# A streamed squared-ReLU down projection: where raw weight chunks, the last gain and the residual lie in SBUF

## The chip, the cores and the metric

One Trainium2 chip, one core. The metric is the time of one execution in microseconds (us): the median of three runs is 1517.41 us (1516.36 to 1518.62).

## The reference, cut to what matters

A decoder layer for 256 tokens, model width 2048, one layer, all in float32. Ahead of the part in question stand the two token mixers (an RG-LRU and a sliding-window attention), whose merged output is added to x. The part that the change touches is the MLP at the end:

```python
h = rmsnorm(x, norm_mlp_pre)                  # (256, 2048)
u = jnp.square(jax.nn.relu(h @ w_mlp_up))     # (256, 8192)
x = x + rmsnorm(u @ w_mlp_down, norm_mlp_post)
```

## The kernel before

**Float32 by halves.** TensorE multiplies a float32 product as three: every operand is split into a high part and a low part (`hi`, `lo`), and hi·hi, hi·lo and lo·hi are accumulated. The weights are read from HBM once, in chunks of 128x2048. `Stream` (`ws`) loads each chunk as two halves of 128x1024 (512 KB) on SP's queue (L76, tile `wraw`), casts the high part on ACT (L94, `whi`) and subtracts on DVE (L95, `wlo`). The raw halves go round a ring of WRAW = 4 buffers, the parts round rings of WHALF = 6. `ahead(j)` asks for the splitting of the halves up to AHEAD (6) on and for loads up to WRAW further on.

**The down projection.** The 8192 inner channels are taken in two halves f = 0, 1 (first the up projection of a half, then its down projection) and the 2048 outputs in two halves n = 0, 1. So there are four passes `down(f, n)` of 16 pairs each; pair p uses one chunk, that is two raw halves. In the first pass pair p has the halves 336 + 2p and the next: `t348`, `tlo352` are of its pairs 6 and 8; pair 0 of the second pass is 368.

An ordinary pair costs 24 matmuls of 128x512. The pairs in `SEVEN` = (0, 2, 4, 6, 8, 10, 12) are done with seven block products in place of eight, as in Strassen's method: 21 matmuls. Their chunk needs sums of its blocks beside the blocks: `split_sums` makes `t` on DVE (L123, L125, L126; L125 overwrites part of the raw half b), ACT casts `thi` (L129), DVE subtracts `tlo` (L130). `t`, `thi` and `tlo` take a room each of the pool `big`: 12 rooms of 8 KB for each partition. In the down passes of f = 0, four of them hold h2T (the input of the up projection) and five hold uT (the activations of ordinary pairs), so three are free; in those of f = 1 h2T is gone, and there are more. The activations of sevenfold pairs lie in seven slots of their own, tag `seven`, that are spent pair by pair in the very last pass.

Within a sevenfold pair TensorE takes the products in the order P1, Q3, P2, P6, Q4 (with T4), Q5 (T1), N7 (T3): the first four use the blocks themselves (12 matmuls), the last three the sums, so the first matmul that reads `tlo` is the 14th. The last two pairs of a pass are held back and finished name by name; behind each name's last matmul stands `finish`.

**The end.** The f = 0 results go to DRAM (`acc_away`) and come back as `acc` for f = 1. In the last pass (f = 1, n = 1) ACT's queue loads the last norm's gain `g3`, spread over 128 partitions (1 MB, L1232), ahead of the pass, and the residual `x1` (2 x 1 MB, L1197) in `early`, behind pair 12. `early` adds `acc` to the partial results (L1193), two of the four on POOL in that pass. `finish` adds the bank (L1210), squares with a sum on ACT (L1214, whose elementwise output goes to a room `spare` that nobody reads) and multiplies with `g3` (L1215); behind the second name of a token tile stand the rms, the update of `x1` (L1223) and the stores (L1224). L1126 is the combination of the seven products behind pair 12.

**Order.** A list scheduler, which simulates the program with costs of its own, sets the order of each engine's instructions; a tile waits for the readers of the tile that had its room or buffer before it. So the order can move wherever a room changes hands.

Of the kernel before, what the change touches and what calls it, by code (L numbers as in the profile page):

```python
# [18 lines left out]
F32 = mybir.dt.float32  # L19
F32R = mybir.dt.float32r  # L20
# [5 lines left out]
P = 128  # L26
# [27 lines left out]
class Stream:  # L54
# [11 lines left out]
    def load_to(self, n):  # L66
        while self.loaded < min(n, 2 * len(self.chunks)):
            j = self.loaded
            c = slice(j % 2 * 1024, j % 2 * 1024 + 1024)
            if j < 2 * EXTRA:  # L70
                if j % 2 == 0:
                    self.place = self.room(f"wraw{j}")
                t = self.place[:, c]
            else:
                t = self.pool.tile([P, 1024], F32, tag="wraw", bufs=WRAW, name=f"wraw{j}")
            self.nc.sync.dma_start(t, self.chunks[j // 2][:, c])  # L76
            self.raw[j] = t
            self.loaded += 1

# [87 lines left out]
def layer(tc, x, g_pre, pos_t, pos_row, inv_freq, vecs, sinks, gains, w_kv, w_q, w_xy, w_rg, w_g, w_rp, w_ap, w_out,  # L167
# [921 lines left out]

    PLACE = {(0, 0): "Q4", (0, 1): "Cs", (1, 0): "P2", (1, 1): "Q3"}  # L1090

    def down(f, n, uT, held, order, finish, early, between=lambda p: None):

        two = [pair(f"s{i}") for i in range(2)]
        banks = {name: two[i // 2][:, i % 2].rearrange("p a b -> p (a b)")
                 for i, name in enumerate(("P1", "P6", "Q5", "N7"))}
        banks.update((name, bank(psb, f"d{name}")) for name in ("P2", "Q3", "Q4", "Cs"))
        begun = set()
        v = nc.vector

        def step(p, parts, names):
            for name in names:
                at, n2 = name
                b = PLACE[name]
                for i, (hi, lo) in enumerate(parts):
                    t = slice(at * P, at * P + P)
                    c = quarter(n2)
                    a = uT[p][:, i]
                    product(banks[b], (a[:, 0, t], a[:, 1, t]), (hi[:, c], lo[:, c]), b in begun,
                            p == PAIRS - 1 and i == 1)  # L1110
                    begun.add(b)

        ready = {}
        for p in range(PAIRS - held):
            if p in SEVEN:
                parts = ws.seven()
# [24 lines left out]
            between(p)  # L1141
        parts = [[ws.half(False) for i in range(2)] for p in range(held)]
        for name in order:
            for i in range(held):
                step(PAIRS - held + i, parts[i], (name,))
            finish(name, banks[PLACE[name]], ready[name])
        ws.ahead(ws.at - 1)

    for f in range(2):
        uT = {}  # L1150
        rooms = [unit(f"uT{f}{i}") for i in range((PAIRS - len(SEVEN) + 1) // 2)]
        full = []
        for p in range(PAIRS):
            u = u2("u")
            if f == 0 and p < 2:
                up_pair(p, wide(u))
            else:
                a_pair(h2T, wide(u), PRIO if p == PAIRS - 1 else 0)
            full.append((p, u))
            if f == 0 and p == R2_AT:  # L1160
                pump(99)
                spread_r2()
                ctx3.close()
                pc = ctx2.enter_context(tc.tile_pool(name="pc", bufs=1))
            if f == 1 or p >= R2_AT:
                for q, u in full:
                    if q in SEVEN:
                        uT[q] = pc.tile([P, 2, 7, P], F32R, tag="seven", bufs=len(SEVEN), name=f"seven{f}{q}")
                    else:
                        i = sum(k not in SEVEN for k in range(q))  # L1170
                        uT[q] = rooms[i // 2][:, 2 * (i % 2) : 2 * (i % 2) + 2]
                    evacuate(q, u, uT[q])
                full.clear()
        order = [(1, 1), (1, 0), (0, 0), (0, 1)]
        if f == 0:
            for n in range(2):
# [11 lines left out]
        x1 = []  # L1188

        def early(ready):  # L1190
            for (tb, i), t in ready.items():
                c = quarter(2 * n + i)
                (nc.gpsimd if n and tb else nc.vector).tensor_tensor(t, t, acc[tb][:, c], ALU.add)  # L1193
            if n == 1:
                for tb in range(TB):
                    x1.append(flat(unit(f"x1{tb}", F32)))
                    nc.scalar.dma_start(x1[tb], x1_away[tb])  # L1197

        def between(p):
            if p in (3, 5, 7, 9):  # L1200
                tb, q = divmod((p - 3) // 2, 2)
                c = quarter(q)
                nc.vector.tensor_tensor(acc[tb][:, c], acc[tb][:, c], g3[:, c], ALU.mult)

        def finish(name, b, t):
            tb, i = name
            q = 2 * n + i
            c = quarter(q)
            a = acc[tb][:, c]
            nc.vector.tensor_tensor(a, b, t, ALU.add)  # L1210
# [3 lines left out]
            nc.scalar.activation(spare[:, c], a, AF.Square, accum_out=sq[:, 3, tb, q : q + 1])  # L1214
            nc.vector.tensor_tensor(t, a, g3[:, quarter(q)], ALU.mult)  # L1215
            last[tb, i] = t
            if i == 0:
                return
            r = rms(tb, 3)
            for q in range(4):  # L1220
                c = quarter(q)
                g = acc[tb][:, c] if q < 2 else last[tb, q - 2]
                nc.vector.scalar_tensor_tensor(x1[tb][:, c], g, r, x1[tb][:, c], ALU.mult, ALU.add)  # L1223
                (nc.scalar if q % 2 else nc.sync).dma_start(o_v[tb][:, c], x1[tb][:, c])  # L1224
# [83 lines left out]
```

## Time and profile before

| what | us |
|---|---|
| median of 3 runs | 1517.41 (1516.36 to 1518.62) |
| the profiled execution | 1517.5 |
| its span | 1515.7 |
| TensorE busy in the span | 1493.5 (99%) |
| DVE busy | 1102.2 (73%) |
| ACT busy | 829.2 (55%) |
| POOL busy | 5.5 |

The profiled execution is the slowest core's; here there is only one. Some 1.8 us lie around the span. Matmul times in the timeline are modelled and overlap (a row says 0.39 where a matmul is issued each 0.23 us), so the pace of TensorE is read from the chain of waits, whose pieces follow on each other.

### The profile page before, as it was taken

How to read it: one execution, taken by the hardware profiler on the slowest of the kernel's cores; microseconds unless marked ns; L12 is line 12 of the kernel's file. 1: busy time of each engine (PE TensorE's matmuls, PEld its weight loads, DVE VectorE, ACT ScalarE, POOL GpSimd, SP SyncE). 2: the span in 40 equal slices, each digit the busy share in tenths (PEclk: the TensorE clock that was granted, in tenths of full speed). 3: DMA queues.
4: the chain of work that ended last, by engine and by line, in shares of the span. 5: the costliest groups of instructions: out<-in, count | busy, mean ns of one | idle time of the engine just before them, and what ended most of it. 6: DMA issues, size and time to landing. Idle time of an engine off the chain costs nothing.

```text
span 1515.7 us, 20016 instructions
## 1 busy us (share of the span) xinstructions
PE 1493.5 (99%) x7600; PEld 1259.8 (83%) x7600; DVE 1102.2 (73%) x1377; ACT 829.2 (55%) x1143; POOL 5.5 (0%) x11
## 2 busy tenths in 40 slices
PE   9999999999999999999999999999999999999996
PEld 7787778788888888888888888888888888888875
DVE  6666677858769966555667866798886666688897
ACT  6554654646566766443355655555454455555543
POOL 0000000000000000000000000000000000000001
PEclk9999999999999999999999999999999999999999
DMA  6645445465646565655764756566657555566564
GB/s 253 218 144 187 142 131 170 153 196 166 217 159 215 174 209 196 191 183 194 268 225 137 271 183 193 185 203 213 219 195 239 194 188 188 193 236 213 195 209 174
DMA packets 82895, 296.19 MB, mean 195 GB/s; under 512 B 9712, under 2 KB 9968, under 8 KB 81648
## 3 DMA queue, kind: packets, MB, share of 16 engines
q1 hardware_dynamic: 79056, 284.43, 57.4%
q10 hardware_dynamic: 3744, 10.50, 1.9%
q8 instruction: 59, 0.97, 0.2%
q14 instruction: 36, 0.29, 0.1%
HBM read 288.60 MB, written 6.29 MB: 195 GB/s over the span
## 4 chain that ended last, share of the span: by engine, by line
PE 82%; DVE 9%; DMA 4%; ACT 2%; issue 2%; DVEq 0%; SPq 0%; ACTq 0%
PE ps L256 21%; PE ps L254 11%; PE dQ L1084 4%; DMA wraw<-in_w_dn 4%; PE pp L294 4%; PE pp L296 4%; PE pp L298 4%; PE g L294 3%; DVE wlo L95 3%; PE g L298 3%; PE g L296 3%; PE s L1084 3%; PE dP L1084 2%; PE q L296 2%; PE q L298 2%; PE q L294 2%
## 5 line engine op out<-in xcount | busy, mean ns | idle before, releaser
L94 ACT CAST whi<-wraw 128x1024 fp32r<-128x1024 f32 x523 | 544.6, 1053 | 567.5 <-PE ps L256 123.7
L95 DVE TENSOR_TENSOR wlo<-wraw,whi 128x1024 fp32r<-128x1024 f32 x523 | 632.8, 1221 | 301.9 <-ACT whi L94 295.2
L256 PE MATMUL ps<-h2T,whi 128*128 128x512 f32 x960 | 223.9, 390 | 0.0
L256 PEld LDWEIGHTS ps<-h2T,whi 128*128 128x128 f32 x960 | 178.2, 188 | 35.6
L256 PE MATMUL ps<-hT,whi 128*128 128x512 f32 x512 | 121.3, 391 | 0.0
L254 PEld LDWEIGHTS ps<-h2T,wlo 128*128 128x128 f32 x960 | 119.1, 192 | 2.3
L254 PE MATMUL ps<-h2T,wlo 128*128 128x256 f32 x960 | 119.9, 283 | 0.0
L256 PEld LDWEIGHTS ps<-hT,whi 128*128 128x128 f32 x512 | 94.7, 188 | 20.1 <-issue 1.5
L1084 PE MATMUL dQ<-whi,uT 128*128 128x512 f32 x288 | 106.9, 389 | 0.0
L294 PE MATMUL g<-whi,hT 128*128 128x512 f32 x256 | 101.2, 395 | 0.0
L296 PE MATMUL g<-wlo,hT 128*128 128x512 f32 x256 | 100.0, 391 | 0.1
L298 PE MATMUL g<-whi,hT 128*128 128x512 f32 x256 | 99.8, 390 | 0.0
L254 PE MATMUL ps<-hT,wlo 128*128 128x256 f32 x512 | 64.9, 283 | 0.0
L254 PEld LDWEIGHTS ps<-hT,wlo 128*128 128x128 f32 x512 | 63.8, 191 | 1.2
L1084 PEld LDWEIGHTS dQ<-whi,uT 128*128 128x128 f32 x288 | 54.1, 188 | 11.2
L1084 PE MATMUL dQ<-wlo,uT 128*128 128x512 f32 x144 | 56.4, 391 | 1.2 <-DVE wlo L95 1.1
L294 PEld LDWEIGHTS g<-whi,hT 128*128 128x128 f32 x256 | 48.1, 188 | 10.6 <-issue 1.0
L298 PEld LDWEIGHTS g<-whi,hT 128*128 128x128 f32 x256 | 48.1, 188 | 10.2
L296 PEld LDWEIGHTS g<-wlo,hT 128*128 128x128 f32 x256 | 48.1, 188 | 9.9 <-DVE wlo L95 0.5
L1084 PE MATMUL dCs<-whi,uT 128*128 128x512 f32 x144 | 54.1, 389 | 0.0
L1084 PE MATMUL dP<-whi,uT 128*128 128x512 f32 x144 | 54.1, 389 | 0.0
L130 DVE TENSOR_TENSOR tlo<-t,thi 128x1536 fp32r<-128x1536 f32 x28 | 49.2, 1756 | 5.5 <-ACT thi L129 5.3
(280 smaller groups left out, 2462.1 us busy)
## 6 DMA issues: line engine op xcount, KB each, us to landing
wraw<-in_w_up SPq DMA_DIRECT2D x128, 512.0 KB, 4.1
wraw<-in_w_dn SPq DMA_DIRECT2D x128, 512.0 KB, 4.8
wraw<-in_w_g SPq DMA_DIRECT2D x64, 512.0 KB, 4.7
wraw<-in_w_xy SPq DMA_DIRECT2D x64, 512.0 KB, 4.5
wraw<-in_w_q SPq DMA_DIRECT2D x32, 512.0 KB, 4.4
wraw<-in_w_ap SPq DMA_DIRECT2D x32, 512.0 KB, 4.6
wraw<-in_w_rp SPq DMA_DIRECT2D x32, 512.0 KB, 4.1
wraw<-in_w_out SPq DMA_DIRECT2D x32, 512.0 KB, 4.9
```

Source lines behind the costliest of these rows:

```text
L94: self.pin(self.nc.scalar.copy(hi, src))
L95: self.pin(self.nc.vector.tensor_tensor(lo, src, hi.bitcast(F32), ALU.subtract))
L130: v.tensor_tensor(lo, t, hi.bitcast(F32), ALU.subtract)
L254: mm(ps[:, f, 1, :], w, a[:, 0, :], start=False, stop=j == 1 and k == 7)
L256: mm(ps[:, f].rearrange("p a b -> p (a b)"), w, a.rearrange("p a b -> p (a b)"), start=kt == 0, stop=j == 3 and k == 7)
L294: mm(banks[tb][n], a[:, 0, t], hi[:, n * 512 : n * 512 + 512], start=first, stop=False)
L296: mm(banks[tb][n], a[:, 0, t], lo[:, n * 512 : n * 512 + 512], start=False, stop=False)
L298: mm(banks[tb][n], a[:, 1, t], hi[:, n * 512 : n * 512 + 512], start=False, stop=last)
L1084: mm(b, a[x], w[y], start=not begun and i == 0, stop=tail and i == 2)
```

## The change

Line numbers of the changed kernel are two higher from the body of `down` on (L1084 is L1086), and more at the end. The diff, cut to its core:

```diff
@@ Stream.load_to
-            if j < 2 * EXTRA:
+            if j < 2 * EXTRA or j // 2 in self.sums:
                 if j % 2 == 0:
                     self.place = self.room(f"wraw{j}")
                 t = self.place[:, c]
...
-            self.nc.sync.dma_start(t, self.chunks[j // 2][:, c])
+            self.load = self.nc.sync.dma_start(t, self.chunks[j // 2][:, c]).ins
@@ Stream.ahead
-        self.load_to(max(2 * EXTRA, j + WHALF) + WRAW)
+        n = max(2 * EXTRA, j + WHALF) + WRAW
+        self.load_to((n + 1) // 2 * 2 + 2 if (n - 1) // 2 in self.sums else n)
@@ down: a callback behind the parts of the held pairs
         parts = [[ws.half(False) for i in range(2)] for p in range(held)]
+        split()
@@ the end, f = 1
-                (nc.gpsimd if n and tb else nc.vector).tensor_tensor(t, t, acc[tb][:, c], ALU.add)
-            if n == 1:
-                for tb in range(TB):
-                    x1.append(flat(unit(f"x1{tb}", F32)))
-                    nc.scalar.dma_start(x1[tb], x1_away[tb])
+                nc.vector.tensor_tensor(t, t, acc[tb][:, c], ALU.add)
+        def free_half(name):
+            t = pc.tile([P, 2, 7, P], F32R, tag="seven", bufs=len(SEVEN), name=name)
+            return t.rearrange("p a b c -> p (a b c)")[:, 0:1024].bitcast(F32)
         def between(p):
-            if p in (3, 5, 7, 9):
+            if p in (0, 2):
+                g3.append(free_half(f"g3{p}"))
+                nc.scalar.dma_start(g3[-1], gains[3][p * 512 : p * 512 + 1024].partition_broadcast(P))
+            if p in (4, 6, 8, 10):
...
+        def residual_back():
+            for tb in range(TB):
+                for i in range(2):
+                    x1[tb, i] = free_half(f"x1{tb}{i}")
+                    with tc.issue_after(ws.load):
+                        ws.load = nc.sync.dma_start(x1[tb, i], x1_away[tb][:, i * 1024 : i * 1024 + 1024]).ins
...
-            nc.scalar.activation(spare[:, c], a, AF.Square, accum_out=sq[:, 3, tb, q : q + 1])
+            nc.scalar.activation(b, a, AF.Square, accum_out=sq[:, 3, tb, q : q + 1])
...
-        spare = flat(unit("spare", F32))
-        g3 = flat(unit("g3", F32))
-        nc.scalar.dma_start(g3, gains[3].partition_broadcast(P))
-        down(f, n, uT, 2, [(0, 0), (0, 1), (1, 0), (1, 1)], finish, early, between)
+        down(f, n, uT, 2, [(0, 0), (0, 1), (1, 0), (1, 1)], finish, early, between, residual_back)
```

In words: (1) both raw halves of a sevenfold chunk lie in one room of `big` instead of two ring buffers, and `ahead` takes such a chunk whole; (2) `g3` comes as two halves into spent `seven` slots, asked for behind pairs 0 and 2 of the last pass, and its multiplications with the first half of `acc` stand one pair later; (3) the residual comes as four loads on SP's queue behind the last weight load, into spent slots; (4) the four adds of the last `early` are all DVE's; (5) the squares' unread output goes to the PSUM bank instead of `spare`.

**Where the order moves: pairs 6 to 8 of the first down pass.** DVE's rows before, from the sums of pair 6 (`t348`) on:

```order
L123 TENSOR_TENSOR t348_8774<-wraw349_8727,wraw348_8713 128x1024
L95 TENSOR_TENSOR wlo348_8781<-wraw348_8713,whi348_8780 128x1024
L125 TENSOR_TENSOR wraw349_8727<-t348_8774,wraw348_8713 128x512
L126 TENSOR_TENSOR t348_8774<-wraw349_8727 128x512
L95 TENSOR_TENSOR wlo349_8785<-wraw349_8727,whi349_8784 128x1024
L95 TENSOR_TENSOR wlo350_8828<-wraw350_8758,whi350_8827 128x1024
L95 TENSOR_TENSOR wlo351_8832<-wraw351_8760,whi351_8831 128x1024
L130 TENSOR_TENSOR tlo348_8776<-t348_8774,thi348_8775 128x1536
L123 TENSOR_TENSOR t352_8851<-wraw353_8804,wraw352_8790 128x1024
```

The same place in the changed kernel:

```order
L95 TENSOR_TENSOR wlo348_8777<-wraw348_8710,whi348_8776 128x1024
L123 TENSOR_TENSOR t348_8770<-wraw348_8710 128x1024
L125 TENSOR_TENSOR wraw348_8710<-t348_8770,wraw348_8710 128x512
L126 TENSOR_TENSOR t348_8770<-wraw348_8710 128x512
L95 TENSOR_TENSOR wlo349_8781<-wraw348_8710,whi349_8780 128x1024
L130 TENSOR_TENSOR tlo348_8772<-t348_8770,thi348_8771 128x1536
L95 TENSOR_TENSOR wlo350_8827<-wraw350_8713,whi350_8826 128x1024
L95 TENSOR_TENSOR wlo351_8831<-wraw351_8715,whi351_8830 128x1024
L95 TENSOR_TENSOR wlo352_8853<-wraw352_8786,whi352_8852 128x1024
L123 TENSOR_TENSOR t352_8846<-wraw352_8786 128x1024
```

`tlo348` moved ahead of pair 7's low parts (350, 351), and the sum `t352` behind `wlo352`. SP's queue at that place before, in plain order of the halves:

```order
L76 DMA wraw348_8713<-in_w_dn 128x1024
L76 DMA wraw349_8727<-in_w_dn 128x1024
L76 DMA wraw350_8758<-in_w_dn 128x1024
L76 DMA wraw351_8760<-in_w_dn 128x1024
L76 DMA wraw352_8790<-in_w_dn 128x1024
L76 DMA wraw353_8804<-in_w_dn 128x1024
```

In the changed kernel (x2 is the two halves of one room):

```order
L76 DMA wraw350_8713<-in_w_dn 128x1024
L76 DMA wraw344_8626<-in_w_dn 128x1024 x2
L76 DMA wraw351_8715<-in_w_dn 128x1024
L76 DMA wraw348_8710<-in_w_dn 128x1024 x2
L76 DMA wraw354_8789<-in_w_dn 128x1024
L76 DMA wraw355_8791<-in_w_dn 128x1024
L76 DMA wraw352_8786<-in_w_dn 128x1024 x2
```

The sevenfold chunks moved behind ordinary halves of later pairs: `wraw352` takes the room of `t348`, which is free when `tlo348` is done, and `t352` takes that of `tlo348`, which is free when TensorE has done pair 6.

**TensorE at pair 8 of that pass.** Before, at its product with T4:

```order
L1084 MATMUL dQ4_8648<-thi352_8852,seven08_7927 128x512
L1084 MATMUL dQ4_8648<-tlo352_8853,seven08_7927 128x512
L1084 MATMUL dQ4_8648<-thi352_8852,seven08_7927 128x512
L1084 MATMUL s1_8645<-thi352_8852,seven08_7927 128x512
L1084 MATMUL s1_8645<-tlo352_8853,seven08_7927 128x512
```

In the changed kernel:

```order
L1086 MATMUL dQ4_8651<-thi352_8847,seven08_7927 128x512
L1086 MATMUL s1_8648<-thi352_8847,seven08_7927 128x512
L1086 MATMUL dQ3_8650<-whi354_8902,uT02_7068 128x512
L1086 MATMUL dP2_8649<-whi354_8902,uT02_7068 128x512
L1086 MATMUL dQ4_8651<-tlo352_8848,seven08_7927 128x512
```

Three matmuls that need no `tlo352` (one of this pair, two of pair 9) moved ahead of the first that does; at pairs 10 and 12 it is four.

**The last pass's end.** SP's last rows before:

```order
L76 DMA wraw526_12573<-in_w_dn 128x1024
L76 DMA wraw527_12575<-in_w_dn 128x1024
L1224 DMA out_0<-x10_12643 128x512 x2
L1224 DMA out_0<-x11_12645 128x512 x2
```

In the changed kernel:

```order
L76 DMA wraw526_12546<-in_w_dn 128x1024
L76 DMA wraw527_12548<-in_w_dn 128x1024
L1218 DMA x100_12648<-x1_away_6224 128x1024
L1218 DMA x101_12650<-x1_away_6224 128x1024
L1218 DMA x110_12652<-x1_away_6224 128x1024
L1218 DMA x111_12654<-x1_away_6224 128x1024
L1240 DMA out_0<-x100_12648 128x512
L1240 DMA out_0<-x101_12650 128x512
```

The residual's loads moved from ACT's queue, where they stood ahead of the last weights' casts, to SP's, behind the last weight loads.

More of the change, by code (lines that the diff above doesn't have):

```diff
@@ L1090, in layer, with down @@
     PLACE = {(0, 0): "Q4", (0, 1): "Cs", (1, 0): "P2", (1, 1): "Q3"}
-    def down(f, n, uT, held, order, finish, early, between=lambda p: None):
+    def down(f, n, uT, held, order, finish, early, between=lambda p: None, split=lambda: None):
         two = [pair(f"s{i}") for i in range(2)]
@@ L1187, in layer @@
             nc.scalar.dma_start(acc[tb], acc_away[tb])
-        x1 = []
+        x1, g3 = {}, []
         def early(ready):
@@ L1192, in early @@
                 c = quarter(2 * n + i)
-                (nc.gpsimd if n and tb else nc.vector).tensor_tensor(t, t, acc[tb][:, c], ALU.add)
-            if n == 1:
-                for tb in range(TB):
-                    x1.append(flat(unit(f"x1{tb}", F32)))
-                    nc.scalar.dma_start(x1[tb], x1_away[tb])
-        def between(p):
-            if p in (3, 5, 7, 9):
-                tb, q = divmod((p - 3) // 2, 2)
-                c = quarter(q)
-                nc.vector.tensor_tensor(acc[tb][:, c], acc[tb][:, c], g3[:, c], ALU.mult)
+                nc.vector.tensor_tensor(t, t, acc[tb][:, c], ALU.add)
+        def free_half(name):
+            t = pc.tile([P, 2, 7, P], F32R, tag="seven", bufs=len(SEVEN), name=name)
+            return t.rearrange("p a b c -> p (a b c)")[:, 0:1024].bitcast(F32)
+        def between(p):
+            if p in (0, 2):
+                g3.append(free_half(f"g3{p}"))
+                nc.scalar.dma_start(g3[-1], gains[3][p * 512 : p * 512 + 1024].partition_broadcast(P))
+            if p in (4, 6, 8, 10):
+                tb, q = divmod((p - 4) // 2, 2)
+                c = quarter(q)
+                nc.vector.tensor_tensor(acc[tb][:, c], acc[tb][:, c], g3[0][:, c], ALU.mult)
+        def residual_back():
[4 more added lines that the diff above has]
+                        ws.load = nc.sync.dma_start(x1[tb, i], x1_away[tb][:, i * 1024 : i * 1024 + 1024]).ins
         def finish(name, b, t):
@@ L1213, in finish @@
                 return
-            nc.scalar.activation(spare[:, c], a, AF.Square, accum_out=sq[:, 3, tb, q : q + 1])
-            nc.vector.tensor_tensor(t, a, g3[:, quarter(q)], ALU.mult)
+            nc.scalar.activation(b, a, AF.Square, accum_out=sq[:, 3, tb, q : q + 1])
+            nc.vector.tensor_tensor(t, a, g3[1][:, quarter(i)], ALU.mult)
             last[tb, i] = t
@@ L1222, in finish @@
                 g = acc[tb][:, c] if q < 2 else last[tb, q - 2]
-                nc.vector.scalar_tensor_tensor(x1[tb][:, c], g, r, x1[tb][:, c], ALU.mult, ALU.add)
-                (nc.scalar if q % 2 else nc.sync).dma_start(o_v[tb][:, c], x1[tb][:, c])
+                y = x1[tb, q // 2][:, quarter(q % 2)]
+                nc.vector.scalar_tensor_tensor(y, g, r, y, ALU.mult, ALU.add)
+                (nc.scalar if q % 2 else nc.sync).dma_start(o_v[tb][:, c], y)
         n = 0
```

## The prediction

> **What bounds the kernel now.** I read the page first, then windows over the down passes, then the chain of waits and the timelines of DVE and ACT in them. From the page, busy time by engine and the shares of the chain that ended last:
>
> ```profile
> PE 1493.5 (99%) x7600; PEld 1259.8 (83%) x7600; DVE 1102.2 (73%) x1377; ACT 829.2 (55%) x1143; POOL 5.5 (0%) x11
> PE 82%; DVE 9%; DMA 4%; ACT 2%; issue 2%; DVEq 0%; SPq 0%; ACTq 0%
> ```
>
> TensorE is idle for 1515.7 − 1493.5 = 22 us in all, so a change that adds no matmul can gain little, and can lose wherever it makes TensorE wait. Windows (length, busy us of PE, PEld, DVE, ACT and POOL, then granted clock, DMA share, GB/s); the first lies in the first down pass, the others in the last:
>
> ```profile
> 1000.00:1025.00 25.00, 25.00 (x112) 20.71 (x111) 22.58 (x21) 12.04 (x11) 0.00 (x0) 1.00 0.71 224
> 1440.00:1445.00 5.00, 4.79 (x22) 3.63 (x21) 3.74 (x4) 2.40 (x3) 0.00 (x0) 1.00 0.77 263
> 1450.00:1455.00 5.00, 4.26 (x19) 3.23 (x18) 5.00 (x6) 3.33 (x4) 0.00 (x0) 1.00 0.75 247
> 1490.00:1495.00 5.00, 4.60 (x19) 3.03 (x17) 3.34 (x5) 3.53 (x4) 0.07 (x1) 1.00 0.22 90
> 1495.00:1500.00 5.00, 4.23 (x19) 3.33 (x19) 4.96 (x6) 0.00 (x0) 3.74 (x2) 1.00 0.00 0
> 1505.00:1510.00 5.00, 0.00 (x0) 0.00 (x0) 4.60 (x9) 1.63 (x5) 0.00 (x0) 0.82 0.62 210
> 1510.00:1515.70 5.70, 0.00 (x0) 0.00 (x0) 2.08 (x4) 0.00 (x0) 0.00 (x0) 0.50 0.55 184
> ```
>
> The first down pass has no idle TensorE at all: nothing is to be gained there, but DVE is busy for 22.58 of 25 us, so what is made later there is late at once. The last pass has gaps of 0.21, 0.74, 0.40 and 0.77 us, then a tail of 10.7 us without matmuls.
>
> The pace, from the chain of waits (start, us, what):
>
> ```profile
> 1007.77 1.36 PE s L1084 x6
> 1017.98 1.36 PE s L1084 x6
> 1065.58 2.72 PE dQ L1084 x12
> ```
>
> Twelve matmuls are 2.72 us, 0.2265 each. The two `s` rows end pairs 2 and 4 (1009.13, 1019.34): two pairs, 45 matmuls, take 10.2 us.
>
> **The raw rooms, first pass.** Nothing is computed anew; what is new is who waits. Before, the raw halves come long ahead in the ring. Now a sevenfold chunk's raw halves wait for the room of the `t` two pairs ahead, free when `tlo` of that pair is done, and its own `tlo` lies behind its load. Three free rooms for raw, `t`, `thi` and `tlo` make this a chain: tlo(p), load of pair p+2, tlo(p+2), from pair 4 on to 12: four links. Its parts are in these rows (the transfers: median us from issue to landing, the third and fourth issued 1.1 us apart, and so the last two):
>
> ```profile
> wraw<-in_w_dn SPq DMA_DIRECT2D x1, 512.0 KB, 3.7
> wraw<-in_w_dn SPq DMA_DIRECT2D x1, 512.0 KB, 3.6
> wraw<-in_w_dn SPq DMA_DIRECT2D x1, 512.0 KB, 3.8
> wraw<-in_w_dn SPq DMA_DIRECT2D x1, 512.0 KB, 5.1
> wraw<-in_w_up SPq DMA_DIRECT2D x1, 512.0 KB, 4.1
> wraw<-in_w_up SPq DMA_DIRECT2D x1, 512.0 KB, 5.6
> ...
> 990.84 1.22 DVE L123 TENSOR_TENSOR t<-wraw,wraw 128x1024 f32<-128x1024 f32 x1
> 992.10 0.69 DVE L125 TENSOR_TENSOR wraw<-t,wraw 128x512 f32<-128x512 f32 x1
> 992.82 0.69 DVE L126 TENSOR_TENSOR t<-wraw 128x512 f32<-128x512 f32 x1
> 1014.06 1.22 DVE L95 TENSOR_TENSOR wlo<-wraw,whi 128x1024 fp32r<-128x1024 f32 x1
> 1019.14 1.49 ACT L129 CAST thi<-t 128x1536 fp32r<-128x1536 f32 x1
> 1020.66 1.76 DVE L130 TENSOR_TENSOR tlo<-t,thi 128x1536 fp32r<-128x1536 f32 x1
> 1022.14 1.06 ACT L94 CAST whi<-wraw 128x1024 fp32r<-128x1024 f32 x1 [1.50 <-PE dCs L1084]
> ```
>
> From tlo(p)'s end to t(p+2)'s start: the first half lands after 3.6 to 3.8 us, then the cast (1.06) and, since DVE's order now has `wlo` of half a ahead of `t`, the subtraction (1.22): 5.9 to 6.1, with 0.3 for the issue and two handovers (my estimate) some 6.3. The second half lands 1.1 + 5.1 = 6.2 or 1.1 + 5.6 = 6.7 behind the first one's issue, so I keep 6.0 to 7.0 and take 6.3. From there: t 1.26 and L125 0.72 (their starts), whi of half b 1.06, thi 1.49, tlo 1.76, with handovers 6.4. A link is 12.7 (12.2 to 13.4) where TensorE needs 10.2: each link falls 2.5 us further behind (2.0 to 3.2), and four of them 10.0 (8.0 to 12.8).
>
> Against this stands a lead at pair 4: t(4) has the room of tlo(2), so it waits for TensorE's end of pair 2 (1009.13), and tlo(4) is there 6.4 later; its first reader stands 24 + 13 matmuls = 8.4 us later: 2.0 us of lead. And the order puts up to four matmuls that need no tlo ahead of the first that does: 0.9. Loss: 10.0 − 2.0 − 0.9 = 7.1 us (5.1 to 9.9). TensorE's late pairs don't hold the links back, since its last product with tlo(p) ends 8 matmuls (1.8 us) behind the first, inside the 6.3 of the load.
>
> [...] The rows of this queue, 3.6 to 3.8 with nothing beside them, are what I take.
>
> **Between the passes.** SP's queue puts the first half of pair 0's raw (368), which waits for tlo(12), ahead of the last held halves 366 and 367. TensorE has 41 matmuls (9.3 us) from that tlo to the first use of wlo367; three transfers (about 6.7 to 8 us, from the pairs above) and 2.3 for cast and subtraction take 9.0 to 10.3: 0.5 us (0 to 1.6).
>
> **Second pass.** The same lead of 2.0 at pair 2 (t waits for the end of pair 0), then one link of 12.7 to pair 4. From pair 6 on a fourth room is there (uT of pairs 1 and 3 is spent), and the raw load waits for `wlo` of half b, some 1.9 ahead of tlo: 10.8, 0.6 too long, twice. 2.5 + 0.6 + 0.6 − 2.0 = 1.7 us (0 to 4.0).
>
> **Passes of f = 1.** h2T's rooms are free, and the raw load of a pair can go out when the pair four ahead ends, 20 us before its use: nothing (0). That room is the cover; with three rooms it would be the first pass again.
>
> **The last pass's gains.** Its gaps are of transfers that collide: the 1 MB of `g3` and the 2 MB of `x1` go out beside the weights' halves, which then take 7.8 and 7.9 us instead of 3.7:
>
> ```profile
> wraw<-in_w_dn SPq DMA_DIRECT2D x1, 512.0 KB, 7.8
> g<-in_gains ACTq DMA_DIRECT2D x1, 1024.0 KB, 8.6
> wraw<-in_w_dn SPq DMA_DIRECT2D x1, 512.0 KB, 7.9
> x<-x_away ACTq DMA_DIRECT2D x1, 1024.0 KB, 6.7
> ...
> 1495.98 0.50 PE L1084 MATMUL dQ<-wlo,uT 128*128 128x512 f32 x1 [0.77 <-DVE wlo L95]
> 1497.76 2.38 DVE L1193 TENSOR_TENSOR t<-t,acc 128x512 f32<-128x512 f32 x2
> 1504.51 0.39 PE L1084 MATMUL dQ<-whi,uT 128*128 128x512 f32 x1
> 1506.84 0.68 DVE L1210 TENSOR_TENSOR acc<-dQ,t 128x512 f32<-128x512 f32 x1
> ```
>
> Now the gain comes in halves behind pairs 0 and 2, and the residual behind the last weights, on their own queue: four loads more on SP, with only the stores behind them, which need what they bring. Its 2 MB would land within 5.2 us at 406 GB/s (the rate of the window below), by about 1497, ten us before the update. So the last weights are no longer late and the four gaps go: 0.21 + 0.74 + 0.40 + 0.77 = 2.1. DVE then has no pile-up at the end either: its last add L1210 starts at 1506.84 though TensorE had ended at 1504.90; it can start some 0.1 behind: 1.8. Gains 3.9 (3.0, if a gap stays, to 4.1).
>
> ```profile
> 1485.00:1490.00 5.00, 5.00 (x24) 4.13 (x22) 1.24 (x2) 1.05 (x1) 0.00 (x0) 1.00 1.00 406
> 1407.91 1.89 DVE L1193 TENSOR_TENSOR t<-t,acc 128x512 f32<-128x512 f32 x3
> 1500.78 0.63 ACT L1214 ACTIVATE spare<-acc 128x512 f32<-128x512 f32 x1 [6.42 <-DVE acc L1210]
> ```
>
> The adds: DVE alone takes 0.63 each (1.89 for three), 2.5 for four, where its two beside POOL's took 2.38: 0.1, and no longer in a pile-up, so nothing. Squares into PSUM instead of `spare`: ACT's 0.63 each stand beside DVE's work; the bank has no later reader: 0 (at worst one such row, 0.6, behind the last add). The multiplications one pair later: the same count, 0.
>
> **Sum.** 7.1 + 0.5 + 1.7 − 2.1 − 1.8 = +5.4 on the profiled execution's 1517.5, which is the median of the runs (1517.41) to 0.1: 1522.9, say 1523. With every bound on the good side 5.1 + 0 + 0 − 4.1 = +1.0, on the bad side 9.9 + 1.6 + 4.0 − 3.0 = +12.5: 1518 to 1530. A measurement of this kernel tells about 0.2%, 3.0 us, from no change: 1514.4 to 1520.4 is "same".
>
> **Rivals.**
> - Faster: the chain of rooms never binds, and only the gains count: 1517.5 − 3.9 = 1513.6. That takes a link of at most 10.2 + 2.9/4 = 10.9 us, so 1.8 less than my sum: transfers would have to land in 2 us, or the raw room come free with `wlo` of half b in the first pass too. For it: the release by `wlo` is what the second pass has from pair 6 on, and it alone is worth the 1.9; against it: with three rooms `tlo` has to take the one that its own raw halves leave, so the room of `t`, free only with `tlo`, is what the next raw halves get, and no row of 512 KB is under 3.6. From a link of 11.6 downward the total is below before.
> - No change: the link is some 11.3 (t starts when both halves have landed, with the handovers smaller and half a's subtraction ahead of landing): 4 × 1.1 − 2.9 + 0.5 − 3.9 = −1.9, 1515.6. For it: TensorE's readers of tlo can be put off a little at each pair; against it: the order has `wlo` of half a ahead of `t`, whatever lands first.
> [...]
>
> **Chances.** Forecast 0.66, faster 0.12, no change 0.17, clock 0.05. Of the forecast some 0.06 lies within 0.2%: faster 0.12, same 0.17 + 0.06 = 0.23, slower 0.60 + 0.05 = 0.65. The range 1515 to 1529 leaves out the faster case (0.12) and the upper end of the forecast and the clock case (0.07). The forecast's own range is 1518 to 1530.
>
> **What would show it.** In the changed kernel's first down pass TensorE waits for DVE's `tlo` at pairs 8, 10 and 12, 2 to 3 us each, none before pair 6; successive tlo ends lie 12.7 us apart; the raw loads wait on SP for DVE. The second pass waits less, for `tlo` or `wlo`; f = 1's first pass not at all. In the last pass the halves land in about 4 us, the gaps are gone, and the last L1210 starts within 0.2 us of the last matmul. I am wrong if the links come out near 10.2, if TensorE's order fills the waits, or if the gains meet a new wait at the end (x1 late).

## The result, and the profile after

The changed kernel takes 1533.42 us (median of four, 1529.12 to 1533.68), where before takes 1516.88 (also a median of four) in the same comparison: the ratio is 1.0113 (1.0100 to 1.0125), 16 to 17 us slower. The forecast was 1523 in a range of 1515 to 1529: the sign came out, the size was three times too small. The profiled execution is 1533.58 (span 1531.8).

From the page, busy time by engine: the same number of matmuls, DVE and ACT as busy as before, TensorE 7 us busier, part of which is a fall of its clock (below).

```profile
span 1531.8 us, 19992 instructions
PE 1500.7 (98%) x7600; PEld 1259.5 (82%) x7600; DVE 1103.1 (72%) x1379; ACT 827.3 (54%) x1143; POOL 1.7 (0%) x9
```

Windows of the changed kernel (length, busy us of PE with its matmuls, PEld, DVE, ACT, POOL, then clock, DMA share, GB/s): the rest of the first down pass, the second, the third, and most of the last:

```profile
1025.00:1075.00 50.00, 45.15 (x185) 35.01 (x184) 36.65 (x33) 23.03 (x23) 0.00 (x0) 0.97 0.50 167
1075.00:1155.00 80.00, 77.37 (x333) 61.56 (x332) 66.44 (x64) 39.77 (x38) 0.00 (x0) 1.00 0.60 198
1350.00:1432.00 82.00, 82.00 (x363) 67.65 (x362) 70.46 (x70) 43.50 (x45) 0.00 (x0) 1.00 0.66 221
1432.00:1505.00 73.00, 70.09 (x305) 56.46 (x304) 61.11 (x58) 36.46 (x38) 0.00 (x0) 1.00 0.55 183
```

The number of matmuls reads best: at full pace 50 us hold 222 and 80 us hold 355 (rows of other kernels below). In the first window 37 are missing, 8.4 us; in the second 22, 5.0 us. The third pass is at full pace.

Counting pairs from the timeline, TensorE falls behind by 8.6 us in the first pass, 5.1 in the second, nothing in the third; the two f = 1 passes together are 1.8 longer than in the first profile of before. The last matmul ends at 1520.87, so the tail without matmuls is 10.9 us, as before (10.8). The start of the first down pass is 0.5 later, which is no effect of the change: in the profiles of this case it lies between 993.4 and 994.9, with nothing changed ahead of it.

The chain is there as drawn. DVE's `tlo` of pairs 4, 6, 8, 10 and 12 (start, duration):

```profile
1013.97 1.76 DVE L130 TENSOR_TENSOR tlo<-t,thi 128x1536 fp32r<-128x1536 f32 x1 [0.15 <-ACT thi L129]
1026.63 1.76 DVE L130 TENSOR_TENSOR tlo<-t,thi 128x1536 fp32r<-128x1536 f32 x1 [0.16 <-ACT thi L129]
1039.21 1.76 DVE L130 TENSOR_TENSOR tlo<-t,thi 128x1536 fp32r<-128x1536 f32 x1
1051.94 1.76 DVE L130 TENSOR_TENSOR tlo<-t,thi 128x1536 fp32r<-128x1536 f32 x1
1064.45 1.76 DVE L130 TENSOR_TENSOR tlo<-t,thi 128x1536 fp32r<-128x1536 f32 x1 [0.16 <-ACT thi L129]
```

They are 12.66, 12.58, 12.73 and 12.51 us apart: the link of 12.7. TensorE meets the lateness earlier in the pair than I had said, at P2, the first product with half b's high and low part, at pairs 8, 10 and 12:

```profile
1037.86 0.49 PE L1086 MATMUL dP<-whi,seven 128*128 128x512 f32 x1 [0.46 <-ACT whi L94]
1039.12 0.50 PE L1086 MATMUL dP<-wlo,seven 128*128 128x512 f32 x1 [0.77 <-DVE wlo L95]
1050.59 0.50 PE L1086 MATMUL dP<-whi,seven 128*128 128x512 f32 x1 [1.21 <-ACT whi L94]
1051.85 0.50 PE L1086 MATMUL dP<-wlo,seven 128*128 128x512 f32 x1 [0.53 <-DVE wlo L95]
1063.10 0.50 PE L1086 MATMUL dP<-whi,seven 128*128 128x512 f32 x1 [1.16 <-ACT whi L94]
1064.35 0.54 PE L1086 MATMUL dP<-wlo,seven 128*128 128x512 f32 x1 [0.53 <-DVE wlo L95]
```

The last pass has a stall that was not forecast, at pair 6:

```profile
1467.65 0.49 PE L1086 MATMUL dP<-whi,seven 128*128 128x512 f32 x1 [1.62 <-ACT whi L94]
1468.91 0.50 PE L1086 MATMUL dP<-wlo,seven 128*128 128x512 f32 x1 [0.76 <-DVE wlo L95]
1470.82 0.50 PE L1086 MATMUL dQ<-tlo,seven 128*128 128x512 f32 x1 [0.26 <-DVE tlo L130]
```

### The profile page after: what moved, and what is told of

It is laid out like the page before. It is cut to its first block, busy times and chain, and to the rows that moved or that the text cites. A ratio compares the mean times of both kernels' runs of the same rounds, so it can differ in the third digit from the quotient of the medians.

```text
span 1531.8 us, 19992 instructions
## 1 busy us (share of the span) xinstructions
PE 1500.7 (98%) x7600; PEld 1259.5 (82%) x7600; DVE 1103.1 (72%) x1379; ACT 827.3 (54%) x1143; POOL 1.7 (0%) x9
## 4 chain that ended last, share of the span: by engine, by line
PE 84%; DVE 7%; DMA 3%; ACT 3%; issue 1%; ACTq 0%; SPq 0%; DVEq 0%
PE ps L258 22%; PE ps L256 11%; PE dQ L1086 6%; PE pp L296 4%; PE pp L298 4%; PE pp L300 4%; PE g L296 3%; PE g L300 3%; PE g L298 3%; DMA wraw<-in_w_dn 3%; PE s L1086 3%; PE dP L1086 3%; PE q L298 2%; PE dCs L1086 2%; PE q L300 2%; PE q L296 2%
## 5 line engine op out<-in xcount | busy, mean ns | idle before, releaser
L1086 PE MATMUL dQ<-whi,uT 128*128 128x512 f32 x288 | 107.1, 390 | 0.0
L1086 PEld LDWEIGHTS dQ<-whi,uT 128*128 128x128 f32 x288 | 54.2, 188 | 11.3 <-ACT whi L94 0.2
L1086 PE MATMUL dQ<-wlo,uT 128*128 128x512 f32 x144 | 56.3, 391 | 0.6 <-DVE wlo L95 0.6
L300 PEld LDWEIGHTS g<-whi,hT 128*128 128x128 f32 x256 | 48.1, 188 | 10.2
L1086 PE MATMUL dP<-whi,uT 128*128 128x512 f32 x144 | 54.3, 391 | 0.0
L1086 PE MATMUL dCs<-whi,uT 128*128 128x512 f32 x144 | 54.3, 391 | 0.0
```

The lines of the kernel that those rows point to most:

```text
L300: mm(banks[tb][n], a[:, 1, t], hi[:, n * 512 : n * 512 + 512], start=False, stop=last)
L1086: mm(b, a[x], w[y], start=not begun and i == 0, stop=tail and i == 2)
```

## The experiments

Ratios are to the kernel before in the same comparison, with their 95% intervals; there, the medians of before are 1513.5 to 1514.6 us.

### Which part of the change costs

**Raw rooms in f = 1 only.**

```diff
-            if j < 2 * EXTRA or j // 2 in self.sums:
+            if j < 2 * EXTRA or j // 2 in self.sums and j // 2 >= self.first:
```

(the same condition in `ahead`; `first` is the first chunk of the f = 1 down passes)

> The changed kernel, but raw rooms only in the two down passes of f = 1; those of f = 0 take the ring as before. Theory (the three-room chain of the f = 0 passes): the traces put 13.6 of the 16.1 us lost into those two passes, so this kernel comes back to 1519 to 1521 us, its f = 0 passes without a TensorE wait, while pair 6 of the last pass still waits about 3 us. Rival A (the end: gain and residual in spent slots, the adds on DVE, the residual on SP's queue): it stays near 1533. Rival B (any raw room costs, f = 0 and f = 1 alike): near 1525.

Measured: 1518.63 us, 1.0032 (1.0020 to 1.0043). Its f = 0 passes have the full count of matmuls:

```profile
1025.00:1075.00 50.00, 50.00 (x222) 41.42 (x221) 41.88 (x42) 24.69 (x23) 0.00 (x0) 1.00 0.63 201
1075.00:1155.00 80.00, 80.00 (x355) 66.24 (x354) 64.70 (x61) 40.38 (x39) 0.00 (x0) 1.00 0.66 221
```

**Raw rooms in f = 0 only** (the condition turned round).

> The changed kernel with raw rooms in the two f = 0 passes only, the ring in f = 1: the complement of the first run. Theory (two separate costs: the three-room chain in f = 0, and the place in SP's queue in the last pass): the loss is the changed kernel's less what the rooms of f = 1 cost (ratios 1.0032 less 1.0003), so 1.0075 to 1.009; 12 to 14 us in the f = 0 passes and none in the last. If the two are not separate (a late first pass shifts the last one), 1.0113 or 1.005.

Measured: 1528.87 us, 1.0087 (1.0073 to 1.0102), as expected. In its profile the f = 0 passes lose 15.4 us, a little more than expected, and the last pass has no wait of over 0.4. So the loss splits into 0.8 to 0.9% for f = 0 and 0.3% for f = 1, and the two add up to the changed kernel's 1.0113 within the intervals.

**The last norm's part alone** (no raw room anywhere: `first` set to the number of chunks).

> The changed kernel without any raw room: the ring of four as before, and only the last norm's part of the change (gain and residual in spent slots, residual on SP behind the last weight load, all four adds on DVE, squares into PSUM). Theory: 1515 to 1517 us, that is 0 to 2 below before, for the held halves land a little earlier, but the residual still shares the transfers of the last half. Rival A: 1525 to 1533. My prediction's terms for this part alone (gaps 2.1 and tail 1.8) would give 1513.

Measured: 1514.15 us, 1.0003 (0.9994 to 1.0012): neither the gain of 3.9 us that my sum had for it nor a loss. Rival A falls. The gaps are gone from its profile, and even so the time is that of before:

```profile
1440.00:1495.00 55.00, 55.00 (x243) 45.30 (x242) 47.18 (x47) 25.81 (x25) 0.00 (x0) 1.00 0.67 221
```

**The raw rooms alone**, put into the kernel before.

> Before with the raw rooms alone; gain, residual, spare and adds as before. Theory: the 13.6 us of the f = 0 passes, and a chain in the last pass too, since gain and spare leave three rooms there as well (another 5 to 8): 1535 to 1539 us. Rival A: 1517 to 1519. Rival B: about 1531.

Measured: 1529.81 us, 1.0110 (1.0094 to 1.0126): the rooms are the whole loss. It is less than expected, though: gain and `spare` in rooms beside them did not make the last pass worse than in the changed kernel. It takes 87.8 us in both profiles, though 1.6 of it is here a fall of the clock behind the waits at pair 6.

### Is it the chain through three rooms?

**tlo taken out of the rooms.** If raw, `t` and `thi` have the three rooms to themselves, no raw load waits for a `tlo`.

```diff
-        hi, lo = [self.room(f"t{part}{j}").bitcast(F32R)[:, 0:1536] for part in ("hi", "lo")]
+        hi = self.room(f"thi{j}").bitcast(F32R)[:, 0:1536]
+        if j // 2 < self.first:
+            lo = self.pool.tile([P, 1024], F32, tag="wraw", bufs=WRAW, name=f"tlo{j}").bitcast(F32R)
+            lo4 = self.small(f"tlo4{j}")
```

(`small` is one 128x512 tile in the pool of the `seven` slots; in f = 1 all is as in the changed kernel)

> The changed kernel with tlo of the f = 0 passes out of the rooms (its T1 and T3 parts in a ring buffer, T4 in 2 KB of its own), so that raw, t and thi have the three rooms to themselves; the subtraction is two instructions instead of one. Theory (the chain tlo, load, sums, tlo through three rooms): the raw load of pair 6 now waits for TensorE's end of pair 2, some 18 us ahead of its use, the waits of the f = 0 passes go (0 to 2 us left of 13.6), and the time is 11 to 13 us below the changed kernel's, as with raw rooms in f = 1 only: ratio to before 1.002 to 1.005. Rival B (it is the rooms' loads, bunched two by two on SP's queue behind later halves, not the third room): the f = 0 waits stay, ratio near 1.011.

Measured: 1519.66 us, 1.0035 (1.0023 to 1.0047). Every wait of the f = 0 passes is gone, although all raw halves still come in rooms, two by two on SP's queue:

```profile
1025.00:1075.00 50.00, 50.00 (x222) 41.40 (x222) 41.94 (x44) 23.39 (x23) 0.00 (x0) 1.00 0.64 215
1075.00:1155.00 80.00, 80.00 (x355) 66.26 (x354) 66.60 (x68) 40.79 (x39) 0.00 (x0) 1.00 0.61 205
```

So it is the third room, not rooms as such: rival B falls.

**A shorter link.** The subtraction of half a's low part is put behind the sums.

```diff
-        v.tensor_tensor(two, b[:, l], b[:, r], ALU.add)
-        ahi, alo = self.two_parts(a, j)
+        last = v.tensor_tensor(two, b[:, l], b[:, r], ALU.add)
+        with self.tc.issue_after(last.ins):
+            ahi, alo = self.two_parts(a, j)
```

> The changed kernel, but DVE makes the sums t of a sevenfold chunk ahead of the low part of its half a (whose subtraction stood in the chain). Theory (each link of the three-room chain adds its excess over 10.2 us): a link is 5.3 us to the landing of the second half, 2.7 for the sums, 2.4 for two low parts and 1.8 for tlo, 12.1 to 12.2 in place of 12.6; six such links then cost 2.5 to 4.5 us less, with the fall of the clock less likely: ratio to before 1.008 to 1.0095 (the changed kernel: 1.0113). Rival (the loss is the loads' own place in SP's queue): ratio unchanged, 1.011.

Measured: 1523.95 us, 1.0068 (1.0056 to 1.0080), a larger gain than expected. Three `tlo` of its first pass (pairs 8, 10, 12):

```profile
1039.09 1.76 DVE L131 TENSOR_TENSOR tlo<-t,thi 128x1536 fp32r<-128x1536 f32 x1
1051.55 1.76 DVE L131 TENSOR_TENSOR tlo<-t,thi 128x1536 fp32r<-128x1536 f32 x1
1063.73 1.76 DVE L131 TENSOR_TENSOR tlo<-t,thi 128x1536 fp32r<-128x1536 f32 x1
```

The links are 12.46 and 12.18, and the f = 0 passes lose 11.3 us in place of 13.7: 2.4 less, just under what the theory gave. Against the kernel with raw rooms in f = 0 only, which loses 15.4 there, it is 4.1 less, inside it. The rest of the gain came from elsewhere: in this kernel SP's order has the load for pair 6 of the last pass ahead of the half of pair 9, not behind it, and the stall there is gone. That is the next point.

### The stall in the last pass

In the order of the changed kernel and of the one with rooms in f = 1, SP's queue has in the last pass (496 is pair 0, 508 pair 6, 514 pair 9; the numbers behind the names are those of the latter kernel):

```
L76 DMA wraw504_12133<-in_w_dn 128x1024 x2
L76 DMA wraw510_12208<-in_w_dn 128x1024
L76 DMA wraw511_12210<-in_w_dn 128x1024
L76 DMA wraw514_12286<-in_w_dn 128x1024
L76 DMA wraw508_12205<-in_w_dn 128x1024 x2
```

The room of pair 6's halves is free when TensorE has done pair 2 (1448.0). But 514 stands ahead of it and waits for a ring buffer, until DVE has made a low part. SP's waits in the changed kernel from 1440 to 1460 (us in total, times, longest), of which this one is the longest:

```profile
SPq L76 <- DVE wlo L95: 16.9, 4, 10.1
```

DVE's row there, two low parts, done at 1454.3:

```profile
1451.97 2.36 DVE L95 TENSOR_TENSOR wlo<-wraw,whi 128x1024 fp32r<-128x1024 f32 x2
```

And the first load of 508, issued at 1454.8, nearly 7 us late, which then takes 7.3 us among the others let go with it, about twice the 3.6 to 3.8 of such a load in before with nothing beside it:

```profile
wraw<-in_w_dn SPq DMA_DIRECT2D x1, 512.0 KB, 7.3
```

**SP's loads kept in the order of use** in f = 1, in the kernel with rooms there:

```diff
-            self.load = self.nc.sync.dma_start(t, self.chunks[j // 2][:, c]).ins
+            with self.tc.issue_after(self.load) if j >= 2 * self.first else ExitStack():
+                self.load = self.nc.sync.dma_start(t, self.chunks[j // 2][:, c]).ins
```

> Raw rooms in f = 1 only, as in the first run, but with SP's loads of those passes kept in the order of use (in that run's last pass the load for pair 6 stands behind a half of pair 9, whose ring buffer came free 7 us after pair 6's room). Theory (the load's place in SP's queue makes the stall of pair 6): the 2 to 3 us stall there goes, ratio to before 1.000 to 1.001 (it was 1.0032). Rival E (DVE and the collisions with the gain's halves make it, the place in the queue does not): 1.002 to 1.004.

Measured: 1513.88 us, 0.9998 (0.9989 to 1.0006). The place of the stall in the kernel with rooms in f = 1:

```profile
1445.00:1460.00 15.00, 13.86 (x60) 10.61 (x59) 12.65 (x12) 6.99 (x7) 0.00 (x0) 1.00 0.54 181
```

The same 15 us in this one, and the start of its third pass:

```profile
1445.00:1460.00 15.00, 15.00 (x68) 12.44 (x67) 13.65 (x13) 7.60 (x7) 0.00 (x0) 1.00 0.69 221
1335.00:1345.00 10.00, 9.05 (x40) 7.18 (x39) 9.52 (x12) 6.58 (x9) 0.00 (x0) 1.00 0.75 238
```

The eight missing matmuls (1.8 us) are back. The place in the queue made the stall; rival E falls. Between the two profiles lie 4.5 us: the stall, 1.5 us at the held pairs and 1.9 of the tail went with it, and in return TensorE waits 0.95 us at pair 0 of the third pass (last row). It does so in both kernels with the order kept over both f = 1 passes and in no other; why was not tried.

### The end

**The residual behind the cast of the last raw half**, on ACT's queue, in the kernel with the last norm's part alone:

```diff
-                    with tc.issue_after(ws.load):
-                        ws.load = nc.sync.dma_start(x1[tb, i], x1_away[tb][:, i * 1024 : i * 1024 + 1024]).ins
+                    with tc.issue_after(ws.cast):
+                        ws.cast = nc.scalar.dma_start(x1[tb, i], x1_away[tb][:, i * 1024 : i * 1024 + 1024]).ins
```

> As the kernel with the last norm's part alone, but the four residual loads stand on ACT's queue behind the cast of the very last raw half, so they start when no weight is under way any more. Theory (from the last subtraction of a low part on, DVE is busy without a break to the end, 17.4 us in both traces, so the end is set by the landing of the last half, which took 7.2 us beside the residual instead of 3.9): 2.5 to 3.5 us below the kernel that loads the residual on SP, 1512 to 1514. Rival C (the tail is set by TensorE's last matmul or by DVE's number of instructions, not by that landing): the same as that kernel to 0.5 us. Rival D: the residual comes too late for the updates, and it is 1 to 4 us slower.

Measured: 1513.49 us, 0.9997 (0.9988 to 1.0006). In the profile the tail is shorter: the last matmul ends at 1503.45, so that 9.1 us are left to the end of the span (1512.6), in place of 11.0 in the kernel with the residual on SP:

```profile
1503.06 0.39 PE L1089 MATMUL dQ<-whi,uT 128*128 128x512 f32 x1
```

DVE's add behind it starts at once:

```profile
1503.51 0.68 DVE L1228 TENSOR_TENSOR acc<-dQ,t 128x512 f32<-128x512 f32 x1
```

But the last half was also issued later than in the kernel it is compared with (1485.0 against 1481.6, of which 1.5 is a later start of the down passes), and TensorE's end with it; the times cannot tell the two kernels apart. The expected 2.5 to 3.5 us did not come.

**The same in the kernel with SP's kept order:**

> The same with the residual behind the cast of the last raw half, on ACT's queue. Where the ring serves only ordinary pairs the last four halves can be loaded earlier. Theory: DVE's work behind the last low part is no longer what ends the kernel, TensorE's last matmul is, 1 to 3 us below the kernel that keeps only SP's order: ratio 0.997 to 1.000. Rival C (no gain at the end): the same as that kernel.

Measured: 1514.13 us, 0.9999 (0.9991 to 1.0008). The tail is 9.1 us in the profile, but so it is in that of the kernel with the residual on SP, and the time is the same: rival C stands here.

**The gain in a room of its own, loaded in the third pass** (`gain_early` issues its halves behind pairs 5 and 9 of n = 0):

```diff
+        def gain_early(p):
+            if p in (5, 9):
+                c = slice(1024 * len(g3), 1024 * len(g3) + 1024)
+                g3.append(room3[:, c])
+                nc.scalar.dma_start(g3[-1], gains[3][c].partition_broadcast(P))
```

> The ring everywhere, the residual behind the cast of the last raw half, and the gain in a room of its own (free now), loaded as two halves behind pairs 5 and 9 of the pass before the last, where no wait of TensorE is to be seen. Theory: no transfer beside weights makes TensorE wait in the last pass, TensorE's end sets the tail (9.1 us instead of 10.8): 1.7 to 2.6 us below before, ratio 0.9982 to 0.9990. Rival: the gaps come with the ring's own pace, not with the gain's load, ratio 0.9992 to 1.0000; or the earlier pass now waits instead, 1.000 or more.

Measured: 1515.92 us, 1.0014 (1.0005 to 1.0023), slower if anything, and widely spread (1512.02 to 1518.88). Its profiled execution is one of its fastest, 1512.20, and has no wait left in the last two passes:

```profile
1336.00:1500.00 164.00, 164.00 (x725) 135.59 (x724) 143.01 (x145) 84.90 (x90) 0.00 (x0) 1.00 0.63 213
```

Where its slower executions lose their 3 to 6 us no trace shows.

**Raw rooms in the last pass alone, in kept order** (`first` one pass later):

> Raw rooms in the last pass alone, SP's loads there in order of use, gain in spent slots, residual behind the cast of the last raw half. Theory: the 1.0 us that the kept order cost at pair 0 of the pass before is gone, the last pass waits 0.5 us or less, the tail is 9.1 us: 1.5 to 2.5 us below before, ratio 0.9984 to 0.9990. Rival: as the kernel with rooms in both f = 1 passes, 0.9999.

Measured: 1514.82 us, 1.0010 (1.0001 to 1.0019). None of these versions beats the kernel before.

**Before, once more**, for a second profile of the gaps that the last norm's part was to remove.

> The kernel before, once more, for a profile on the chip of these runs: the kernel with only the last norm's part had a profile 3.2 us shorter than the first profile of before in the down passes of f = 1, while the timed runs of both agree. If the gain is real and something else takes it back, this profile shows the same gaps as the first one in the last pass (1.3 us at pairs 4 and 6, 1.7 us in the held steps); if the gaps of before differ from run to run, it shows smaller ones.

Measured: 1514.76 us in one run. Two windows in which the first profile of before shows gaps of 0.21 and 0.74 us:

```profile
1440.00:1445.00 5.00, 5.00 (x23) 4.13 (x22) 3.38 (x4) 1.12 (x2) 0.00 (x0) 1.00 0.79 283
1450.00:1455.00 5.00, 5.00 (x23) 3.96 (x22) 5.00 (x5) 1.55 (x2) 0.00 (x0) 1.00 0.72 238
```

And the one wait of over 0.2 us that TensorE has in its last pass:

```profile
1493.24 0.50 PE L1084 MATMUL dQ<-wlo,uT 128*128 128x512 f32 x1 [0.76 <-DVE wlo L95]
```

The gaps at pairs 4 and 6 are not there: they are not in every execution of this kernel. Whether the execution or the chip makes them is open: the median of before is 1516.9 us in the comparison with the changed kernel and 1513.5 to 1514.6 in the later ones, and the changed kernel was timed in the first alone.

## Why the prediction was wrong

These steps failed: the terms for f = 1 (raw rooms at nothing, gaps −2.1, tail −1.8), where +1.9 us was measured in place of −3.9, which is 5.8 of the 10.7 us between the sum and the measurement; and the lead that I gave the second pass, which was not there, 2.9. The chain of the first pass was right.

**Right: the mechanism and the link.** Three rooms make a chain of `tlo`, load, sums, `tlo`; a link was 12.5 to 12.7 us (12.7 forecast) against TensorE's 10.2, and taking `tlo` out of the rooms takes the loss of f = 0 away. From the end of tlo(8) to the start of t(10) it is 6.4 us in the changed kernel (1040.97 to 1047.38), where I had 6.3; the 0.3 in it for the issue and two handovers was an estimate that no row shows. The third pass costs nothing, as said.

**First pass, 7.1 forecast, 8.6 measured.** Within its bounds, but not by the parts of my sum alone: at pair 12 the clock fell, to which I had given a chance of 0.05; no run of before shows when that happens while matmuls run, or what it costs. For 3.4 us the granted clock is 0.50:

```profile
1064.67:1068.09 3.42, 3.42 (x9) 2.65 (x8) 3.42 (x3) 3.42 (x4) 0.00 (x0) 0.50 0.20 48
```

The matmuls there start 0.43 us apart in place of 0.2265; eight such steps are 1.6 us, so the waits alone are 7.0. That this is the forecast's 7.1 is partly luck: I had reckoned the lead at the first product with `tlo` and taken off 0.9 for the matmuls moved ahead of it, and from pair 8 on the waits stand at P2. Nor would the pass have been 1.6 shorter without the fall. In the kernel with raw rooms in f = 0 only the clock does not fall (1.00 from 1025 to 1075), and this pass loses 9.1 us all the same, since TensorE then waits for the low parts of the held halves:

```profile
1074.82 0.50 PE L1087 MATMUL dQ<-wlo,uT 128*128 128x512 f32 x1 [0.76 <-DVE wlo L95]
```

This is the wait that I had forecast between the passes (0.5). It is some 1.6 us there, counted by the starts of the matmuls, and none in the changed kernel.

**Between the passes and second pass, 0.5 + 1.7 forecast, 5.1 measured.** The step that failed is "the same lead of 2.0 at pair 2". I took it from the room of `t` alone and left out the link ahead of it, pair 0 to pair 2, whose raw load waits for tlo(0). Here it is, DVE's `tlo` of pairs 0, 2 and 4:

```profile
1084.18 1.74 DVE L130 TENSOR_TENSOR tlo<-t,thi 128x1536 fp32r<-128x1536 f32 x1
1097.56 1.76 DVE L130 TENSOR_TENSOR tlo<-t,thi 128x1536 fp32r<-128x1536 f32 x1 [0.16 <-ACT thi L129]
1110.42 1.76 DVE L130 TENSOR_TENSOR tlo<-t,thi 128x1536 fp32r<-128x1536 f32 x1 [0.15 <-ACT thi L129]
```

tlo(0) starts 19.7 us behind tlo(12), 7 more than a link. Most of this is SP's queue again: the second half of pair 0 stands behind the held halves 366 and 367, goes out 2.65 us after the first half and takes 8.5 us. So the sums of pair 0 start 11.4 us behind the end of tlo(12), where a forecast link had 6.3:

```profile
wraw<-in_w_dn SPq DMA_DIRECT2D x1, 512.0 KB, 8.5
1077.64 1.22 DVE L123 TENSOR_TENSOR t<-wraw 128x1024 f32<-128x1024 f32 x1
```

The rest is DVE, which has three of the four adds of the first pass's end (L1183) among its instructions there. The next link is 13.4. With the lead used up, pair 2 is already late by 0.9, pair 4 adds 2.1, and pairs 6 and 8, over the fourth room, 0.6 and 1.0 (0.6 each forecast; their links are 10.74 and 10.82, as forecast).

**Last pass, raw rooms at nothing.** "The raw load of a pair can go out when the pair four ahead ends": the room could, the queue could not. I had noted which room each load waits for and not what stands ahead of it on SP: a half for three pairs later, waiting for a ring buffer. It is 2.6 us of wait at pair 6, and some 0.3% with the rest that rooms cost in f = 1.

**The gaps, −2.1.** Mis-sized: of the four gaps only the last, of 0.77, is in the other profile of before too (0.76). Against that profile, whose last pass is 2.4 us shorter than the first one's, the changed kernel's last pass is 4.2 longer and not 1.8. And the edit did not free the last halves of company: the last one still lands late, since SP issues the residual right behind it. The changed kernel's chain of waits, its last transfer:

```profile
1502.31 7.17 DMA wraw<-in_w_dn
```

With the last norm's part alone the last half takes 8.0 us, and with the residual put behind its cast 4.9:

```profile
wraw<-in_w_dn SPq DMA_DIRECT2D x1, 512.0 KB, 8.0
wraw<-in_w_dn SPq DMA_DIRECT2D x1, 512.0 KB, 4.9
```

These rows, 7.2 and 8.0 us for half a megabyte issued ahead of 2 MB on its own queue and 4.9 without them, show that being first in the queue did not keep this transfer's time to itself.

**The tail, −1.8.** I had DVE's last adds starting with TensorE's end. In the changed kernel they do not: from the last low part on, DVE works almost without a break, and TensorE's end is not what it waits for:

```profile
1510.64 1.22 DVE L95 TENSOR_TENSOR wlo<-wraw,whi 128x1024 fp32r<-128x1024 f32 x1 [2.53 <-ACT whi L94]
1514.18 1.88 DVE L1196 TENSOR_TENSOR t<-t,acc 128x512 f32<-128x512 f32 x3
1515.98 0.68 DVE L1225 TENSOR_TENSOR acc<-dQ,t 128x512 f32<-128x512 f32 x1
```

From that low part to the last update's end it is 17.4 us, before and after alike, so in this profile the late half, 7.2 us after its issue, is where the stretch to the end begins. But the place of the residual does not decide how long the tail is. The kernel with SP's kept order and the one with the sums first have it on SP's queue too, and tails of 9.1 us. In the former DVE has 21 instructions from the last low part on, in the changed kernel 28, and it waits for TensorE:

```profile
1496.95 0.69 DVE L1228 TENSOR_TENSOR acc<-dCs,t 128x512 f32<-128x512 f32 x1 [1.32 <-PE dCs L1089]
```

So 1.8 us less of tail is what a DVE without a pile-up leaves, as I had it, but the edit did not remove the pile-up; and where the tail was shorter by the residual's place alone, no shorter time could be measured.

In sum, of the 10.7 us between +5.4 and the profiled execution's +16.1, 2.9 are the second pass, some 1.5 the first one with the clock, 0.5 the start, and the other 5.8 the f = 1 passes and the tail, where I had −3.9 and got +1.9.

## What to carry to other kernels

When buffers are shared, follow the ring all the way round: which room does the next load take, whose last reader frees it, and is the trip from there back to that reader longer than the pace of the engine that must not wait; a lead holds only once, and each link of the ring has to be asked in turn. Then read the issuing queue as well as the room: a load whose room is free still waits behind whatever stands ahead of it, and in an order that a scheduler set by its own costs, a load went out 7 us late on the chip. And before a gap is booked as a gain, look at a second profile of the same kernel: of 2.1 us of gaps here 1.4 were absent in the second.

## What the runs showed of the hardware

TensorE's clock fell after waits of 1.16 and 0.53 us in the changed kernel, of 1.28 and 0.53 and again of 0.87 and 0.76 in the kernel with the raw rooms alone, and of 1.64 and 0.77 in the one with tlo taken out. In the changed kernel the granted clock was 0.50 for 3.41 us (1064.68 to 1068.09), in which eight matmuls started 0.43 us apart, and 1.6 us was lost. A window inside the first fall of the kernel with the raw rooms alone, and one around that of the kernel with tlo taken out, where matmuls start 0.43 us apart as well:

```profile
1053.00:1056.00 3.00, 3.00 (x9) 2.33 (x8) 3.00 (x3) 1.03 (x2) 0.00 (x0) 0.50 0.33 74
1455.00:1460.00 5.00, 5.00 (x16) 3.94 (x15) 5.00 (x6) 2.60 (x3) 0.00 (x0) 0.66 0.20 69
```

Waits of the same size did not do it elsewhere: 1.21 and 0.53 at pair 10 of the changed kernel, 1.62, 0.76 and 0.26 in its last pass, both at a clock of 1.00.

Here are the 3.41 us just ahead of the four falls, one of the changed kernel, two of the one with the raw rooms alone and one of that with tlo taken out; TensorE is busy for 1.00 to 1.78 us of them:

```profile
1061.26:1064.67 3.41, 1.72 (x6) 0.81 (x6) 2.70 (x4) 2.67 (x3) 0.00 (x0) 1.00 0.04 16
1049.32:1052.73 3.41, 1.60 (x6) 0.87 (x6) 2.70 (x4) 3.02 (x3) 0.00 (x0) 1.00 0.00 0
1465.75:1469.16 3.41, 1.78 (x7) 0.92 (x6) 2.71 (x4) 3.15 (x3) 0.00 (x0) 1.00 0.06 23
1451.64:1455.05 3.41, 1.00 (x4) 0.50 (x4) 2.71 (x4) 2.71 (x3) 0.00 (x0) 1.00 0.04 16
```

Stretches of the same length in the changed kernel, at pair 10 of its first pass and at pair 6 of its last, have no more, and no fall behind them:

```profile
1048.50:1051.91 3.41, 1.67 (x7) 0.73 (x6) 2.71 (x4) 2.42 (x3) 0.00 (x0) 1.00 0.01 4
1465.50:1468.91 3.41, 1.02 (x5) 0.27 (x3) 2.77 (x4) 2.36 (x3) 0.00 (x0) 1.00 0.13 54
```

So neither the size of the waits nor how busy TensorE is just ahead tells the falls from the rest here; what does is not settled. All this is read from four falls, and the busy times are modelled.
